# Tile 0 in two transfers with eight gains ahead, four zero writes behind the tables, and the ones-matmuls of the first norm behind the first token tile

## The chip, the cores and the metric

The kernel runs on one core of one Trainium2 chip. The metric is device time in microseconds (us) of one execution; of three runs of the kernel before, the median is 1820.84 us, the lowest 1819.13 and the highest 1823.46.

## What is computed

Two layers of a transformer block over 512 tokens of 1024 channels, in float32. Each layer normalises its input, projects it with one wide matrix into three kinds of attention and gates, merges them, and runs a squared-ReLU MLP; only the first norm and the first projections matter here:

```python
def _rms_norm(x, g):
    x32 = x.astype(jnp.float32)
    y = x32 * lax.rsqrt(jnp.mean(x32 * x32, axis=-1, keepdims=True) + NORM_EPS)
    return (y * g.astype(jnp.float32)).astype(x.dtype)
...
    for l in range(DEPTH):
        h = _rms_norm(x, attn_norm[l])
        proj = h @ w_in[l]
        a_q, a_k, a_v, b_ql, b_kvl, b_kr, c_q, c_k, c_v, gate = jnp.split(proj, IN_SPLITS, axis=-1)

        aq = _partial_rope(_rms_norm(a_q.reshape(grp), a_q_norm[l]), cos_p, sin_p)
        ak = _partial_rope(_rms_norm(a_k.reshape(grp), a_k_norm[l]), cos_p, sin_p)
        o_a = _dilated_mixture(aq, ak, a_v.reshape(grp)).reshape(B, S, DSA_OUT)
...
        x = x + merged @ w_out[l]

        h2 = _rms_norm(x, mlp_norm[l])
        x = x + jnp.square(jax.nn.relu(h2 @ w_ff1[l])) @ w_ff2[l]
    return x
```

## The kernel before

`x` lies transposed: eight tiles of 128 channels by 512 tokens. Every float32 matmul is made of three (`mm3`): both operands are split into a rounded high part and the rest, and high x high (L339), high x low (L340) and low x high (L341) are summed in one accumulator. Weights come in chunks through the SP queue into `raww` (two buffers); ACT casts a chunk to its high part `hl` (three buffers) and DVE subtracts to get the low part, both at a raised priority. The very first chunk is loaded and split in two halves of 128x512.

The norm is not applied ahead of the projection. `norm_tile` multiplies each tile by its gain and splits it (`a`), and sums the squares over the eight tiles in one tile. `norm_steps` splits that sum, multiplies it by a matrix of ones on TensorE (L458, L459, "the ones-matmuls", into `pso`), adds the epsilon on DVE (L461, `tmp`), picks the diagonals out of it (`dg` and `sm`, L468: a custom DVE operation on `tmp` and `ident`) and takes the reciprocal root on ACT and DVE (L358 to L362). The result `rcol` has one factor per token; it scales the projections when ACT empties their accumulators ("evacuations", `raw<-psd,rcol`).

The first projection (`denseB`, queries and keys of the first attention) takes four chunks of weights, each with two channel tiles: 24 matmuls of 512 columns a chunk, over four token tiles with an accumulator each, two of tag d and two of tag s. In its last chunk, the ones-matmuls stand behind token tile `npos`. Each of the four accumulators is emptied twice (two copies of `raw`), so eight evacuations follow. The next projection (288 columns, three channel tiles in its first two chunks) uses tags d, d, d and o; as there are three accumulators of tag d, its second one of tag d needs one that the first projection has given back.

Tile 0 comes with all gains of both layers in one transfer on the ACT queue (128x938 values). Its two operations on DVE are L434 and L435; the other tiles use ACT and DVE (L350, L351). GpSimd (POOL in the profile) writes zeros into the unused halves of the two block diagonal key tiles (`kbd_open`: four casts, L573 and L574, `kT<-zero`), and multiplies the rope tables by gains (L553, `tqb`, `tkb`, `tqn`, `tkn`, `tqr`, `tkr`), which needs the transfer of `ropes`.

Each engine runs its instructions in program order. That order is made when the program is built, by a scheduler that takes what is ready, by priority; `high_priority` raises it, and `issue_after` holds an instruction back in the order until another has been placed.

Of the kernel before, what the change touches and what calls it, by code (L numbers as in the profile page):

```python
# [8 lines left out]
F32 = mybir.dt.float32  # L9
# [3 lines left out]
ALU = mybir.AluOpType  # L13
# [3 lines left out]
P = 128  # L17
L = 2
D = 1024
S = 512  # L20
KT = D // P
NT = S // P
# [141 lines left out]
NG = 21 + 192  # L164
# [91 lines left out]
class Kern:  # L256
# [124 lines left out]
    def setup(self, es):  # L381
        tc, nc = self.tc, self.nc
        self.cp = es.enter_context(tc.tile_pool(name="cp", bufs=1))
        self.kp = es.enter_context(tc.tile_pool(name="kp", bufs=1))
        self.pp = es.enter_context(tc.tile_pool(name="pp", bufs=2, space=PSUM))
        self.wsetup()
        self.x = []
        k = lambda shape, nm, dt=F32: self.kp.tile(shape, dt, name=nm, tag=nm)
        self.bcol = k([96, L, 2], "bcol")
        self.warm(k)  # L390
        x0 = k([P, S + L * NG], "x0")
        nc.scalar.dma_start(x0, self.ins["x0g"])
        nc.scalar.add_instruction(
            mybir.InstLoadActFuncSet(name=nc.get_next_instruction_name(), act_func_set_id=ACT_SET, ins=[], outs=[])
        )
        self.gain = x0[:, S:].rearrange("p (l n) -> p l n", l=L)
        self.x.append(x0[:, :S])
        self.wload(1)
        for j in range(1, KT):
            xt = self.t(self.cp, "x2", [P, S])  # L400
            nc.sync.dma_start(xt, self.ins["xT"][j])
            self.x.append(xt)
            if j == 1:
                self.wload(2)
        self.ident = k([P, P], "ident")
        self.ropes = k([P, NROPE], "ropes")
        self.masks = k([P, NMASK], "masks", BF16)
        self.maskA = self.masks[:, C_MA : C_MA + 256]
        self.maskR = self.masks[:, C_MR : C_MR + 256]
        self.maskB = self.masks[:, C_MB : C_MB + 512]  # L410
        self.resetC = self.masks[:, C_MC : C_MC + 512]
# [16 lines left out]
    def norm_tile(self, j, x):  # L428

        nc = self.nc  # L430
        g = self.gain[:, self.gl, self.goff + j : self.goff + j + 1]
        hl = self.t(self.cp, "a4", [P, 2, S], F32R)
        if j == 0 and self.gl == 0 and self.goff == 0:
            nc.vector.tensor_scalar(hl[:, 0], x, g, None, ALU.mult)  # L434
            nc.vector.scalar_tensor_tensor(hl[:, 1], x, g, hl[:, 0].bitcast(F32), ALU.mult, ALU.subtract)  # L435
        else:
            self.split(hl[:, 0], hl[:, 1], x, g)
        self.xg[j] = hl
        first = self.nacc is None
        if first:  # L440
            self.nacc = self.t(self.cp, "x2", [P, S])
        sq = self.nacc if first else self.t(self.cp, "tmp", [P, S])
        nc.scalar.activation(sq, x, AF.Square)
        if not first:
            nc.vector.tensor_tensor(self.nacc, self.nacc, sq, ALU.add)
# [5 lines left out]
    def norm_steps(self, cols):  # L451

        nc = self.nc
        hl = self.t(self.cp, "a4", [P, 2, S], F32R)
        self.split(hl[:, 0], hl[:, 1], self.nacc)
        yield
        ps = self.ps("o")
        nc.tensor.matmul(ps, self.onesr, hl[:, 0], start=True, stop=False)  # L458
        nc.tensor.matmul(ps, self.onesr, hl[:, 1], start=False, stop=True)  # L459
        a = self.t(self.cp, "tmp", [P, S])  # L460
        nc.vector.tensor_scalar(a, ps, 1.0 / D, EPS, ALU.mult, ALU.add)  # L461
        if cols:
            self.rcol = self.kp.tile([P, 8], F32, tag="rcol", name=self.nm("rcol"))
            c = self.small()
            for i in range(2):
                for t in range(NT):
                    sl = slice(t, None, 4) if i else slice(t * P, t * P + P)
                    nc.vector.tensor_tensor_reduce(  # L468
                        out=self.t(self.kp, "dg", [P, P]), in0=a[:, sl], in1=self.ident, op0=ALU.mult, op1=ALU.add,
                        scale=1.0, scalar=0.0, accum_out=c[:, 4 * i + t : 4 * i + t + 1],  # L470
                    )
                self.rsqrt(self.rcol[:, 4 * i : 4 * i + 4], c[:, 4 * i : 4 * i + 4], self.kp, "sm8", [P, 4])
        self.rrep = self.kp.tile([P, S], F32, tag="rrep", name=self.nm("rrep"))
        self.rsqrt(self.rrep, a, self.cp, "tmp", [P, S])
# [14 lines left out]
    def denseB(self, names, nk, n, evac, res=False, tags="dddo", last=None):  # L489

        pss = [self.ps(tags[t]) for t in range(NT)]
        k0 = 0
        for name, m in zip(names, nk):
            fin = last if name is names[-1] else None
            if fin is not None:
                next(fin)
                if self.gl:
                    for _ in fin:
                        pass
                    fin = None  # L500
            w = self.wget(name)
            for t in range(NT):
                sl = slice(t, None, 4) if res else slice(t * P, t * P + P)
                for kk in range(m):
                    xg = self.xg[k0 + kk]
                    c = kk * n
                    self.mm3(
                        pss[t][:, :n], xg[:, 0, sl], xg[:, 1, sl], w[:, 0, c : c + n], w[:, 1, c : c + n],
                        k0 + kk == 0, k0 + kk == KT - 1,
                    )  # L510
                if fin is not None and t == self.npos:
                    for _ in fin:
                        pass
                if k0 + m == KT and (fin is None or t >= self.npos):
                    for u in range(t + 1) if fin is not None and t == self.npos else (t,):
                        evac(u, pss[u])
            k0 += m


# [25 lines left out]
    def rope_tab(self, base, hf, grow, tag, pool=None):  # L545

        nc = self.nc
        w = 2 * hf  # L550
        src = self.ropes[:, base : base + 8 * w].rearrange("p (t c) -> p t c", t=4)
        t = (pool or self.tp).tile([P, 4, 2 * w], F32, tag=tag, name=self.nm(tag))
        nc.gpsimd.tensor_tensor(t, src, grow.unsqueeze(1).to_broadcast([P, 4, 2 * w]), ALU.mult)  # L553
        return t[:, :, 0:w], t[:, :, w : 2 * w]

    def to_qT(self, y, g, d=P):
# [239 lines left out]
    def layer(self, l):  # L796
        nc, tc = self.nc, self.tc
        st = {}
        g = lambda a, b: self.gain[:, l, a:b]
# [15 lines left out]
        def thread_A():  # L815
            with tc.tile_pool(name=f"ta{l}", bufs=1) as tp:
# [2 lines left out]
                tabs["kn"] = self.rope_tab(R_N, 8, g(53, 85), "tkn")  # L819
                tabs["qr"] = self.rope_tab(R_R, 8, g(21, 53), "tqr")  # L820
                tabs["kr"] = self.rope_tab(R_R, 8, g(53, 85), "tkr")
                self.kbd_open(2)
                yield ("open", "A")
                oA = [self.t(self.cp, "a4", [P, 2, S], F32R) for _ in range(2)]
                st["oA"] = oA
# [438 lines left out]
        for name, cost, fn, need in items:  # L1264
# [10 lines left out]
            while credit > 0:  # L1275
                c = step()
# [18 lines left out]
        for q in range(4):  # L1295
            u = []
# [32 lines left out]
        return self.ins["xT"][j] if l == 0 else self.park[j]  # L1329

    nwarm = 8
    npos = 2
    ratio = 0.8
    w0at = (0, 2, 4)
    srtmp = True
# [50 lines left out]
```

## Time and profile before

| | |
|---|---|
| median of three runs | 1820.84 us |
| profiled execution | 1820.94 us |
| its span, first to last instruction | 1819.1 us |
| granted TensorE clock, mean | 1.000 |
| four zero writes on POOL | 1.94 to 6.25 us |
| first real matmul | 6.68 us |
| first matmul of the next projection | 30.39 us |
| six tables on POOL | 22.68 to 25.47 us |

The profile is of one execution. Its page gives the busy time of each engine and the chain that ended last; the trace also answers with timelines (start and duration of each instruction, in us from the start of the span, and in brackets how long its engine stood idle before it and what ended that), with the waits of an engine, and with busy times in chosen stretches. PE is TensorE, and a matmul's duration overlaps with the next one's, so rates are read from the distance of their starts.

### The profile page before, as it was taken

The page shows a single profiled execution, that of the slowest core. Times are in us where ns is not written, and L with a number is a line of the kernel's source. Part 1 is how long each engine was busy: PE and PEld are TensorE (multiplying, and loading weights), DVE is VectorE, ACT ScalarE, POOL GpSimd, SP SyncE. Part 2 cuts the span into 40 slices and gives each one's busy share as a digit, 9 for nine tenths or more (in the row PEclk, how much of TensorE's full clock was granted, in tenths as well). Part 3 has the DMA queues.
Part 4 walks back from the last instruction along what each step waited for, and adds up shares of the span by engine and source line. Part 5 has one row for each costly group of instructions (what it writes and reads, how often), then busy time and mean ns, then how long its engine had stood idle before and what let it go on. Part 6 is the DMA issues. An engine that isn't in the chain of part 4 may idle for free.

```text
span 1819.1 us, 23060 instructions
## 1 busy us (share of the span) xinstructions
PE 1798.3 (99%) x8592; PEld 1511.8 (83%) x8592; DVE 1158.5 (64%) x2137; ACT 929.8 (51%) x1743; POOL 41.3 (2%) x70
## 2 busy tenths in 40 slices
PE   9999999999999999999999999999999999999999
PEld 8999888777788888888889988887778888888887
DVE  7666799868875443434566558997888654434342
ACT  6646677767744332323446366677767342323241
POOL 1000000000000000000020000000000000000000
PEclk9999999999999999999999999999999999999999
DMA  5222241223353233233432222423234532333332
GB/s 180 83 94 86 65 134 60 97 95 109 116 184 100 93 96 102 93 99 99 133 102 83 91 70 71 133 64 105 93 116 124 171 94 93 101 96 93 104 94 93
DMA packets 64704, 186.78 MB, mean 103 GB/s; under 512 B 11472, under 2 KB 11856, under 8 KB 64592
## 3 DMA queue, kind: packets, MB, share of 16 engines
q1 hardware_dynamic: 57744, 178.35, 30.8%
q0 software_dynamic: 1952, 6.29, 1.0%
q8 instruction: 68, 1.11, 0.2%
q10 hardware_dynamic: 4896, 0.66, 0.2%
q14 instruction: 44, 0.36, 0.1%
HBM read 168.45 MB, written 16.78 MB: 102 GB/s over the span
## 4 chain that ended last, share of the span: by engine, by line
PE 86%; DVE 8%; ACT 4%; issue 1%; DMA 1%; ACTq 0%; SPq 0%; DVEq 0%
PE psd L486 21%; PE psd L485 21%; PE psd L484 21%; PE psd L339 3%; PE psd L341 3%; PE psd L340 3%; PE pst L761 2%; DVE SN L978 1%; PE pss L339 1%; PE pss L340 1%; PE pss L341 1%; DVE hl L251 1%; PE pss L970 1%; PE pst L561 1%; PE pso L742 1%
## 5 line engine op out<-in xcount | busy, mean ns | idle before, releaser
L251 ACT CAST hl<-raww 128x1024 fp32r<-128x1024 f32 (+3 forms) x287 | 298.7, 1041 | 648.4 <-PE psd L486 482.5
L484 PE MATMUL psd<-a,hl 128*128 128x512 f32 x1232 | 484.9, 394 | 0.6 <-DVE VS L251 0.5
L485 PE MATMUL psd<-a,hl 128*128 128x512 f32 x1232 | 484.4, 393 | 0.0
L486 PE MATMUL psd<-a,hl 128*128 128x512 f32 x1232 | 484.4, 393 | 0.0
L251 DVE TENSOR_TENSOR hl<-raww,hl 128x1024 fp32r<-128x1024 f32 (+3 forms) x287 | 347.5, 1211 | 150.8 <-ACT hl L251 150.4
L484 PEld LDWEIGHTS psd<-a,hl 128*128 128x128 f32 x1232 | 231.9, 188 | 45.0 <-DVE VS L251 1.1
L485 PEld LDWEIGHTS psd<-a,hl 128*128 128x128 f32 x1232 | 231.7, 188 | 44.5 <-issue 0.3
L486 PEld LDWEIGHTS psd<-a,hl 128*128 128x128 f32 x1232 | 231.8, 188 | 44.2
L486 PE MATMUL psd<-u,hl 128*128 128x512 f32 (+1 forms) x648 | 250.7, 387 | 0.0
L485 PE MATMUL psd<-u,hl 128*128 128x512 f32 (+1 forms) x648 | 250.7, 387 | 0.0
L484 PE MATMUL psd<-u,hl 128*128 128x512 f32 (+1 forms) x648 | 250.7, 387 | 0.0
L1319 DVE TENSOR_TENSOR x<-x,psd 128x512 f32<-128x512 f32 x63 | 43.3, 688 | 185.0 <-PE psd L486 185.0
L484 PEld LDWEIGHTS psd<-u,hl 128*128 128x128 f32 x648 | 121.8, 188 | 24.7
L485 PEld LDWEIGHTS psd<-u,hl 128*128 128x128 f32 x648 | 121.8, 188 | 24.6
L486 PEld LDWEIGHTS psd<-u,hl 128*128 128x128 f32 x648 | 121.8, 188 | 24.5
L1300 DVE SCALAR_TENSOR_TENSOR tmp<-psd,rrep 128x512 f32<-128x512 f32 x64 | 44.3, 692 | 151.4 <-PE psd L486 151.4
L339 PE MATMUL psd<-hl,a 128*128 128x512 f32 (+3 forms) x328 | 122.6, 375 | 4.5 <-DVE gt L251 2.2
L340 PE MATMUL psd<-hl,a 128*128 128x512 f32 (+3 forms) x328 | 122.0, 372 | 0.0
L341 PE MATMUL psd<-hl,a 128*128 128x512 f32 (+3 forms) x328 | 121.6, 371 | 0.0
L251 ACT ACTIVATE gt<-gt 128x512 f32<-128x512 f32 x144 | 90.0, 628 | 25.5 <-DVE gt L251 20.1
L339 PEld LDWEIGHTS psd<-hl,a 128*128 128x128 f32 x328 | 79.4, 242 | 9.9 <-DVE gt L251 3.0
L340 PEld LDWEIGHTS psd<-hl,a 128*128 128x128 f32 x328 | 79.5, 243 | 3.7
(234 smaller groups left out, 2403.3 us busy)
## 6 DMA issues: line engine op xcount, KB each, us to landing
raww<-w SPq DMA_DIRECT2D x277, 512.0 KB, 3.5
gpark<-gt SPq DMA_DIRECT2D x48, 256.0 KB, 2.3
gt<-gpark SPq DMA_DIRECT2D x48, 256.0 KB, 3.7
x<-xT POOLq DMA_DIRECT2D x8, 256.0 KB, 4.1
park<-x POOLq DMA_DIRECT2D x8, 256.0 KB, 2.3
x<-park POOLq DMA_DIRECT2D x8, 256.0 KB, 3.7
x<-xT SPq DMA_DIRECT2D x7, 256.0 KB, 5.8
outT<-x SPq DMA_DIRECT2D x7, 256.0 KB, 2.0
```

The lines of the kernel that those rows point to most:

```text
L251: return f(*a, **k)
L339: mm(ps, ah, bh, start=start, stop=False)
L340: mm(ps, ah, bl, start=False, stop=False)
L341: mm(ps, al, bh, start=False, stop=stop)
L484: self.nc.tensor.matmul(o, w[:, 0, c : c + P], t[:, 0], start=k == 0, stop=False)
L485: self.nc.tensor.matmul(o, w[:, 0, c : c + P], t[:, 1], start=False, stop=False)
L486: self.nc.tensor.matmul(o, w[:, 1, c : c + P], t[:, 0], start=False, stop=k == last)
L561: nc.tensor.transpose(ps[:d, t * P : t * P + P], y[:, t], self.ident)
L742: mm(po[a, r::4], vr[r // 2][:, r % 2, 2 * hh + g], prs[r // 2][:, c : c + P], start=False, stop=False)
L761: nc.tensor.transpose(ps[:, kt * P : kt * P + P], s[:, kt * P : kt * P + P], self.ident)
L1300: nc.vector.scalar_tensor_tensor(t, ps, 0.0, self.rrep, ALU.max, ALU.mult)
L1319: nc.vector.tensor_tensor(x, x, ps, ALU.add)
```

## The change

The host array `x0g` holds the eight gains of the first norm of layer 0 and then tile 0 (128x520). It is loaded in two transfers, 128x264 and 128x256, both on the ACT queue. All gains come in a transfer of their own (`gain`, 128x426) on the SP queue, behind the last token tile. The two DVE operations on tile 0 are made for each half of its columns. The four zero writes of layer 0 are held back behind the last of the six tables (in layer 1 their order was so already). `npos` is 0, the other token tiles of the last chunk are held back behind the ones-matmuls, and the evacuations are written behind the loop.

```diff
--- before.py
+++ after.py
@@ -388,13 +388,15 @@
         k = lambda shape, nm, dt=F32: self.kp.tile(shape, dt, name=nm, tag=nm)
         self.bcol = k([96, L, 2], "bcol")
         self.warm(k)
-        x0 = k([P, S + L * NG], "x0")
-        nc.scalar.dma_start(x0, self.ins["x0g"])
+        x0 = k([P, KT + S], "x0")
+        self.cut = KT + S // 2
+        for c in (slice(0, self.cut), slice(self.cut, KT + S)):
+            nc.scalar.dma_start(x0[:, c], self.ins["x0g"][:, c])
         nc.scalar.add_instruction(
             mybir.InstLoadActFuncSet(name=nc.get_next_instruction_name(), act_func_set_id=ACT_SET, ins=[], outs=[])
         )
-        self.gain = x0[:, S:].rearrange("p (l n) -> p l n", l=L)
-        self.x.append(x0[:, :S])
+        self.gain0 = x0[:, :KT]
+        self.x.append(x0[:, KT:])
         self.wload(1)
         for j in range(1, KT):
             xt = self.t(self.cp, "x2", [P, S])
@@ -402,6 +404,8 @@
             self.x.append(xt)
             if j == 1:
                 self.wload(2)
+        self.gain = k([P, L, NG], "gain")
+        nc.sync.dma_start(self.gain, self.ins["gain"])
         self.ident = k([P, P], "ident")
         self.ropes = k([P, NROPE], "ropes")
         self.masks = k([P, NMASK], "masks", BF16)
@@ -428,11 +432,13 @@
     def norm_tile(self, j, x):
 
         nc = self.nc
-        g = self.gain[:, self.gl, self.goff + j : self.goff + j + 1]
+        start = self.gl == 0 and self.goff == 0
+        g = self.gain0[:, j : j + 1] if start else self.gain[:, self.gl, self.goff + j : self.goff + j + 1]
         hl = self.t(self.cp, "a4", [P, 2, S], F32R)
-        if j == 0 and self.gl == 0 and self.goff == 0:
-            nc.vector.tensor_scalar(hl[:, 0], x, g, None, ALU.mult)
-            nc.vector.scalar_tensor_tensor(hl[:, 1], x, g, hl[:, 0].bitcast(F32), ALU.mult, ALU.subtract)
+        if start and j == 0:
+            for c in (slice(0, S // 2), slice(S // 2, S)):
+                nc.vector.tensor_scalar(hl[:, 0, c], x[:, c], g, None, ALU.mult)
+                nc.vector.scalar_tensor_tensor(hl[:, 1, c], x[:, c], g, hl[:, 0, c].bitcast(F32), ALU.mult, ALU.subtract)
         else:
             self.split(hl[:, 0], hl[:, 1], x, g)
         self.xg[j] = hl
@@ -456,7 +462,7 @@
         yield
         ps = self.ps("o")
         nc.tensor.matmul(ps, self.onesr, hl[:, 0], start=True, stop=False)
-        nc.tensor.matmul(ps, self.onesr, hl[:, 1], start=False, stop=True)
+        self.sqprod = nc.tensor.matmul(ps, self.onesr, hl[:, 1], start=False, stop=True)
         a = self.t(self.cp, "tmp", [P, S])
         nc.vector.tensor_scalar(a, ps, 1.0 / D, EPS, ALU.mult, ALU.add)
         if cols:
@@ -499,6 +505,7 @@
                         pass
                     fin = None
             w = self.wget(name)
+            pin = ExitStack()
             for t in range(NT):
                 sl = slice(t, None, 4) if res else slice(t * P, t * P + P)
                 for kk in range(m):
@@ -511,9 +518,12 @@
                 if fin is not None and t == self.npos:
                     for _ in fin:
                         pass
-                if k0 + m == KT and (fin is None or t >= self.npos):
-                    for u in range(t + 1) if fin is not None and t == self.npos else (t,):
-                        evac(u, pss[u])
+                    pin.enter_context(self.tc.issue_after(self.sqprod.ins))
+                if k0 + m == KT and fin is None:
+                    evac(t, pss[t])
+            pin.close()
+            for t in range(NT) if fin is not None else ():
+                evac(t, pss[t])
             k0 += m
 
 
@@ -550,7 +560,7 @@
         w = 2 * hf
         src = self.ropes[:, base : base + 8 * w].rearrange("p (t c) -> p t c", t=4)
         t = (pool or self.tp).tile([P, 4, 2 * w], F32, tag=tag, name=self.nm(tag))
-        nc.gpsimd.tensor_tensor(t, src, grow.unsqueeze(1).to_broadcast([P, 4, 2 * w]), ALU.mult)
+        self.lastrope = nc.gpsimd.tensor_tensor(t, src, grow.unsqueeze(1).to_broadcast([P, 4, 2 * w]), ALU.mult)
         return t[:, :, 0:w], t[:, :, w : 2 * w]
 
     def to_qT(self, y, g, d=P):
@@ -819,7 +829,8 @@
                 tabs["kn"] = self.rope_tab(R_N, 8, g(53, 85), "tkn")
                 tabs["qr"] = self.rope_tab(R_R, 8, g(21, 53), "tqr")
                 tabs["kr"] = self.rope_tab(R_R, 8, g(53, 85), "tkr")
-                self.kbd_open(2)
+                with tc.issue_after(self.lastrope.ins):
+                    self.kbd_open(2)
                 yield ("open", "A")
                 oA = [self.t(self.cp, "a4", [P, 2, S], F32R) for _ in range(2)]
                 st["oA"] = oA
@@ -1329,7 +1340,7 @@
         return self.ins["xT"][j] if l == 0 else self.park[j]
 
     nwarm = 8
-    npos = 2
+    npos = 0
     ratio = 0.8
     w0at = (0, 2, 4)
     srtmp = True
@@ -1369,7 +1380,8 @@
     arrays = {
         "xT": xT,
         "w": _pack_weights(a["w_in"], a["w_q_b"], a["w_kv_b"], a["w_branch"], a["w_out"], a["w_ff1"], a["w_ff2"]),
-        "x0g": np.concatenate([xT[0], gain.reshape(P, -1)], axis=1),
+        "x0g": np.concatenate([gain[:, 0, :KT], xT[0]], axis=1),
+        "gain": gain,
         "bcol": _pack_bcols(a["b_q_norm"], a["b_k_norm"]),
         "ident": np.eye(P, dtype=np.float32),
         "ropes": _ropes(),
```

On TensorE, in the last chunk of the first projection; before (`psd` and `pss` are the accumulators of the four token tiles, `hl` the weights, `a4` the channel tiles):

```order
L339 MATMUL pss_45_202<-hl_47_228,a4_27_157 128x512
L340 MATMUL pss_45_202<-hl_47_228,a4_27_157 128x512
L341 MATMUL pss_45_202<-hl_47_228,a4_27_157 128x512
L339 MATMUL pss_45_202<-hl_47_228,a4_29_163 128x512
L340 MATMUL pss_45_202<-hl_47_228,a4_29_163 128x512
L341 MATMUL pss_45_202<-hl_47_228,a4_29_163 128x512
L458 MATMUL pso_53_310<-a4_50_284,onesr_69 128x512
L459 MATMUL pso_53_310<-a4_50_284,onesr_69 128x512
L339 MATMUL pss_46_203<-hl_47_228,a4_27_157 128x512
L340 MATMUL pss_46_203<-hl_47_228,a4_27_157 128x512
L341 MATMUL pss_46_203<-hl_47_228,a4_27_157 128x512
L339 MATMUL pss_46_203<-hl_47_228,a4_29_163 128x512
```

And now, with the first six of the eighteen matmuls that used to stand ahead:

```order
L341 MATMUL psd_43_205<-hl_47_233,a4_27_162 128x512
L339 MATMUL psd_43_205<-hl_47_233,a4_29_168 128x512
L340 MATMUL psd_43_205<-hl_47_233,a4_29_168 128x512
L341 MATMUL psd_43_205<-hl_47_233,a4_29_168 128x512
L464 MATMUL pso_53_303<-a4_50_289,onesr_69 128x512
L465 MATMUL pso_53_303<-a4_50_289,onesr_69 128x512
L339 MATMUL psd_44_206<-hl_47_233,a4_27_162 128x512
L340 MATMUL psd_44_206<-hl_47_233,a4_27_162 128x512
L341 MATMUL psd_44_206<-hl_47_233,a4_27_162 128x512
L339 MATMUL psd_44_206<-hl_47_233,a4_29_168 128x512
L340 MATMUL psd_44_206<-hl_47_233,a4_29_168 128x512
L341 MATMUL psd_44_206<-hl_47_233,a4_29_168 128x512
```

The ones-matmuls (`onesr`) moved 12 matmuls up, behind the first token tile.

On TensorE, where the next projection (`x288`) takes the accumulator of tag d that the first one must give back (`psd_115`), 33 matmuls into it before:

```order
L339 MATMUL pso_117_514<-hl_51_287,a4_19_134 128x288
L340 MATMUL pso_117_514<-hl_51_287,a4_19_134 128x288
L341 MATMUL pso_117_514<-hl_51_287,a4_19_134 128x288
L339 MATMUL pso_117_514<-hl_51_287,a4_21_140 128x288
L340 MATMUL pso_117_514<-hl_51_287,a4_21_140 128x288
L341 MATMUL pso_117_514<-hl_51_287,a4_21_140 128x288
L339 MATMUL psd_115_512<-hl_48_255,a4_11_109 128x288
L340 MATMUL psd_115_512<-hl_48_255,a4_11_109 128x288
L341 MATMUL psd_115_512<-hl_48_255,a4_11_109 128x288
```

and 17 matmuls into it now:

```order
L339 MATMUL pso_117_519<-hl_48_260,a4_14_124 128x288
L340 MATMUL pso_117_519<-hl_48_260,a4_14_124 128x288
L341 MATMUL pso_117_519<-hl_48_260,a4_14_124 128x288
L339 MATMUL pso_117_519<-hl_48_260,a4_16_130 128x288
L340 MATMUL pso_117_519<-hl_48_260,a4_16_130 128x288
L339 MATMUL psd_115_517<-hl_48_260,a4_11_112 128x288
L340 MATMUL psd_115_517<-hl_48_260,a4_11_112 128x288
L341 MATMUL psd_115_517<-hl_48_260,a4_11_112 128x288
L339 MATMUL psd_115_517<-hl_48_260,a4_14_124 128x288
```

The accumulator is taken 16 matmuls sooner; what stood ahead of it, chunk `hl_51` among it, stands behind it.

On GpSimd, from its first cast on, before:

```order
L573 CAST kT_39_192<-zero_65 64x2x512
L574 CAST kT_39_192<-zero_65 64x2x512
L573 CAST kT_40_195<-zero_65 64x2x512
L574 CAST kT_40_195<-zero_65 64x2x512
L553 ISA
L553 TENSOR_TENSOR tqb_33_177<-ropes_103,x0_80 128x256
L553 TENSOR_TENSOR tkb_34_179<-ropes_103,x0_80 128x256
L553 TENSOR_TENSOR tqn_35_184<-ropes_103,x0_80 128x128
L553 TENSOR_TENSOR tkn_36_186<-ropes_103,x0_80 128x128
L553 TENSOR_TENSOR tqr_37_188<-ropes_103,x0_80 128x128
L553 TENSOR_TENSOR tkr_38_190<-ropes_103,x0_80 128x128
```

and now:

```order
L563 TENSOR_TENSOR tqb_33_182<-ropes_106,gain_103 128x256
L563 TENSOR_TENSOR tkb_34_184<-ropes_106,gain_103 128x256
L563 TENSOR_TENSOR tqn_35_189<-ropes_106,gain_103 128x128
L563 TENSOR_TENSOR tkn_36_191<-ropes_106,gain_103 128x128
L563 TENSOR_TENSOR tqr_37_193<-ropes_106,gain_103 128x128
L563 TENSOR_TENSOR tkr_38_195<-ropes_106,gain_103 128x128
L583 CAST kT_39_197<-zero_65 64x2x512
L584 CAST kT_39_197<-zero_65 64x2x512
L583 CAST kT_40_200<-zero_65 64x2x512
L584 CAST kT_40_200<-zero_65 64x2x512
L720 CAST PT_243_1433<-zero_65 128x2x128
```

The four zero writes moved from ahead of the six tables to behind them.

## The prediction

> **What bounds the kernel now.** I read the page first: busy shares, then the chain that ended last.
>
> ```profile
> span 1819.1 us, 23060 instructions
> PE 1798.3 (99%) x8592; PEld 1511.8 (83%) x8592; DVE 1158.5 (64%) x2137; ACT 929.8 (51%) x1743; POOL 41.3 (2%) x70
> PE 86%; DVE 8%; ACT 4%; issue 1%; DMA 1%; ACTq 0%; SPq 0%; DVEq 0%
> ```
>
> TensorE is busy for 99% of the span, so the kernel is bound by its matmuls, and whatever keeps TensorE from its next matmul is paid in full. The profiled execution took 1820.94 us, 1.8 us more than its span; the median of the runs is 1820.84 us, 0.1 less, so I add my sum to 1820.94. The order of the program differs only in its first part (some 300 of 7,890 rows on TensorE), so next I asked for TensorE's waits in the first 100 us.
>
> ```profile
> PE psd L339 <- ACT hl L251: 1.8, 1, 1.8
> PE psd L339 <- ACT raw L251: 0.5, 1, 0.5
> PE psd L484 <- DVE VS L251: 0.5, 1, 0.5
> ```
>
> There are three waits (us in total, times, longest): at the first real matmul, at one that needs an emptied accumulator of the first projection, and at the first matmul of the other form (weights stationary, L484) behind it. Nothing that the change does can take away more than these and what the clock costs at the start. The timeline of TensorE places the first two, and shows the rates I need:
>
> ```profile
> 6.68 1.19 PE L339 MATMUL psd<-hl,a 128*128 128x512 f32 x2 [1.84 <-ACT hl L251]
> 7.67 0.63 PE L339 MATMUL pss<-hl,a 128*128 128x512 f32 x1
> 8.09 1.06 PE L340 MATMUL psd<-hl,a 128*128 128x512 f32 x2
> ...
> 9.71 0.39 PE L340 MATMUL pss<-hl,a 128*128 128x512 f32 x1
> 9.93 0.39 PE L341 MATMUL psd<-hl,a 128*128 128x512 f32 x1
> ...
> 13.58 0.39 PE L339 MATMUL psd<-hl,a 128*128 128x512 f32 x1
> ...
> 28.78 0.39 PE L459 MATMUL pso<-a,onesr 128*128 128x512 f32 x1
> ...
> 30.39 0.29 PE L339 MATMUL psd<-hl,a 128*128 128x288 f32 x1
> ...
> 34.63 0.29 PE L341 MATMUL pso<-hl,a 128*128 128x288 f32 x1
> 35.42 0.40 PE L339 MATMUL psd<-hl,a 128*128 128x288 f32 x1 [0.49 <-ACT raw L251]
> ```
>
> Columns are start, duration, instruction, and in brackets the wait. From 7.67 to 8.09 a 512-column matmul takes 0.42 us, from 9.71 to 9.93 only 0.22 (0.228 on the mean of the 16 steps from 9.93 to 13.58): TensorE ran at half speed until about 9.6. The first 24 end at 13.58. From 30.39 to 34.63 lie 32 steps of 288 columns, 0.1325 each.
>
> **Part 1: an earlier start.** The first matmul waits for its weights (ACT's cast) and for tile 0 times its gains (DVE's L434); the rows are from the timelines of ACT, GpSimd (POOL) and DVE, the last from the DMA issues (KB, us to landing):
>
> ```profile
> 4.98 0.62 ACT L251 CAST hl<-raww 128x512 fp32r<-128x512 f32 x1 [2.50 <-DMA raww<-w]
> ...
> 5.21 1.04 POOL L574 CAST kT<-zero 64x1024 fp32r<-64x1024 f32 x1
> ...
> 5.29 1.24 DVE L434 TENSOR_SCALAR a<-x 128x512 fp32r<-128x512 f32 x1 [4.03 <-DMA x<-x0g]
> ...
> 53.54 0.42 DVE L251 TENSOR_SCALAR gt<-gt 128x512 f32<-128x512 f32 x1
> ...
> x<-x0g ACTq DMA_DIRECT2D x1, 469.0 KB, 4.5
> ```
>
> The cast ends at 5.60. L434 took 1.24 us where a tensor_scalar of the same size takes 0.42: it began under the last of the four zeros on GpSimd (to 6.25) and ended 0.28 after it. The change removes both things: no zero stands there, and half a tile (0.42 / 2) lands sooner, as 132 KB go ahead instead of 469. So the cast is what ends last, and the first matmul starts near 5.6, 1.0 to 1.1 us sooner. If TensorE comes to full speed at the same instant, 9.6, then 1.06 us at half speed are worth 0.5 us. If the shorter idle time ahead of it brings full speed as early as 6.2, two matmuls run at half speed until 6.5 and 22 behind them take 22 x 0.228 = 5.0, so the 24 end near 11.5 instead of 13.58: 2.1 us. I take 1.3, between the two. The additional instructions (two more on DVE, one issue on ACT, one gain transfer on SP behind the last token tile) are under DVE's backlog and the full queues; the bytes ahead of the third weight chunk are the same in sum, 132 + 128 + 213 KB. If that cover is gone they cost the half-tile instructions' fixed time, some 0.2 us.
>
> **Part 2: product of squares 12 matmuls sooner.** The two ones-matmuls move from behind 18 matmuls of the last chunk to behind 6: 12 x 0.228 = 2.7 us. With part 1 the second ends at 29.17 - 2.7 - 1.3 = 25.2. Without anything else in the way the DVE chain behind it would follow as it does now:
>
> ```profile
> 17.16 0.68 DVE L445 TENSOR_TENSOR x<-x,tmp 128x512 f32<-128x512 f32 x1
> ...
> 25.66 1.07 DVE L251 TENSOR_TENSOR hl<-raww,hl 128x864 fp32r<-128x864 f32 x1 [2.76 <-ACT hl L251]
> 29.20 0.69 DVE L461 TENSOR_SCALAR tmp<-pso 128x512 f32<-128x512 f32 x1 [2.48 <-PE pso L459]
> 29.93 0.29 DVE L468 CUSTOM_DVE_ANT_0 dg<-tmp,ident 128x128 f32<-128x128 f32 x1
> ...
> 31.59 0.75 DVE L251 TENSOR_TENSOR hl<-raww,hl 128x576 fp32r<-128x576 f32 x1
> ...
> 33.61 0.16 DVE L362 SCALAR_TENSOR_TENSOR rcol<-sm,sm 128x4 f32<-128x4 f32 x1
> ```
>
> It takes 4.6 us from L461 to rcol at 33.77, with a weight split of 0.75 us inside it. In the new order the split of 1.07 falls there in its place, so I count 4.9: rcol at about 30.1, 3.7 us sooner.
>
> **Part 3: what must wait for it moves up.** With all evacuations behind the loop, TensorE meets the accumulator that the fourth evacuation frees 16 matmuls sooner, 16 x 0.1325 = 2.1 us of work that now stands behind the wait instead of ahead of it.
>
> ```profile
> 33.80 0.47 ACT L251 ACTIVATE raw<-psd,rcol 128x256 f32<-128x256 f32 x1 [1.63 <-DVE rcol L362]
> ```
>
> Before, rcol at 33.77 released TensorE at 35.42: 1.65 later (four evacuations). So the new release, carried to the same matmul, is rcol + 1.65 + 2.1; it is 35.42 when rcol is 31.65. Everything queued behind that matmul on TensorE waits too. The third wait above (0.5, for a DVE result) goes when TensorE arrives later. The whole change is therefore **rcol - 31.65 - 0.5**.
>
> **Part 4: the zeros behind the tables.** They leave the start, but come to lie here:
>
> ```profile
> 22.68 0.71 POOL L553 TENSOR_TENSOR tqb<-ropes,x 128x256 f32<-128x256 f32 x1 [16.43 <-DMA masks<-masks]
> ...
> 25.43 0.39 POOL L710 CAST PT<-zero 128x256 fp32r<-128x256 f32 x1
> ```
>
> The tables still start with the rope transfer, 22.68, and end near 25.45; then come four zeros of 1.04, so GpSimd is busy from 22.7 to 29.7 at least, just when DVE works on the chain of part 2. What that does was seen at L434, and layer 1, whose order is already tables then zeros, shows it again:
>
> ```profile
> 914.75 1.50 POOL L573 CAST kT<-zero 64x1024 fp32r<-64x1024 f32 x1
> ...
> 915.28 1.52 DVE L445 TENSOR_TENSOR x<-x,tmp 128x512 f32<-128x512 f32 x1
> ...
> 918.70 1.69 DVE L251 TENSOR_TENSOR hl<-raww,hl 128x1024 fp32r<-128x1024 f32 x1 [0.29 <-ACT hl L251]
> 919.35 1.94 POOL L574 CAST kT<-zero 64x1024 fp32r<-64x1024 f32 x1
> ```
>
> The L445 of 915.28 (0.68 alone, by the row of 17.16) ends 0.55 after the zero ahead of it, which ends at 916.25; the zero of 919.35 (1.04 alone) ends 0.9 after the DVE operation of 918.70, which ends at 920.39. They take turns, whole instructions at a time. There it costs nothing, since TensorE did not wait. Here each zero can hold the chain once. Nothing shows whether the `dg` operations and the 4-column ones are held. If all are: dg, zero, dg, zero, dg, zero, weight split, zero, dg and so on from 25.45, rcol at 34.2, 4.1 late. If only the long ones are, three zeros meet a waiting DVE operation (the split and two of 0.68) with some 0.6 us of theirs to go: rcol at 32.0, 1.9 late. Less than nothing it cannot be, as no zero does work for this chain; nothing at all is the first rival. I take 33.5, nearer the upper end, as the L434 row and the layer-1 rows held every DVE operation that they met. Sum: 33.5 - 31.65 - 0.5 = **+1.35**, and between the two ends -0.15 and +2.05.
>
> The Trainium skill, "SBUF — State Buffer", section "SBUF: two separate sides", calls the port pair of GpSimd and DVE an exclusive lock held for a whole instruction, also by a DVE operation with two SBUF inputs. The rows above agree with it (1.24 us against 0.42); by it `dg`, which reads two tiles, is held too, and the sum would be +2.05.
>
> **The rivals.** *Little contention (faster).* rcol at 30.1 lets TensorE wait about half a microsecond only, and the start's gain stays: 30.1 - 31.65 - 0.5 = -2.05, between -1.2 and -2.9 with the start's two ends (0.5 and 2.1 in place of 1.3): 1818.9. For it: two-input work is only part of the chain. Against it: the rows of layer 1. The point from which it decides is rcol at 32.15.
>
> *The clock falls in the wait (slower).* In the forecast TensorE, which would be at its waiting matmul at 34.63 + 0.13 - 2.1 - 1.3 = 31.4, stands until 33.5 + 1.65 = 35.15, some 3.8 us, where the longest wait after the start is now 1.26:
>
> ```profile
> 1815.23:1818.64 3.41, 0.41 (x4) 0.20 (x2) 0.42 (x1) 0.00 (x0) 0.00 (x0) 1.00 0.11 38
> 1818.64:1819.10 0.46, 0.00 (x0) 0.00 (x0) 0.00 (x0) 0.00 (x0) 0.00 (x0) 0.50 0.00 0
> ...
> 203.52 0.33 PE L704 MATMUL pst<-ident,SN 128*128 128x128 f32 x1 [1.26 <-DVE SN L605]
> ```
>
> The first two rows are windows at the program's end (busy time of PE, PEld, DVE, ACT, POOL, then the granted clock): after 3.41 us with only 0.41 of TensorE's work the clock fell to 0.50. The wait of 1.26 in the last row did not lower it. 3.8 us lie nearer the first. At half speed for half to one and a half such stretches behind the wait, 1.7 to 5.2 us, TensorE loses 0.9 to 2.6, mean 1.7: 1.35 + 1.7 = +3.1, 1824.0, and up to +4.7. It decides from a wait of about 3.4 us. The Trainium skill, "TensorE: Matmul & The Clock Gate", Part 1, gives one idle window of about 3.4 us, on a grid that runs freely, as what halves the clock; the first two rows agree with that length, 3.41. By it a wait of 3.8 us seldom holds a whole idle window, and the sum would stay at +1.35.
>
> *The start does not come sooner,* because the cast or its transfer is later than I think. With the chain held by GpSimd the sum has no term of the start left, so the time is the forecast's, 1822.3.
>
> **How the numbers follow.** Forecast, chain held and clock kept: 0.52 (with the start that stays put in it), 1820.94 + 1.35 = 1822.3, own range 1820.4 to 1823.2. Little contention: 0.25, 1818.9. Clock falls: 0.23, 1824.0. The runs of before lie 4.3 us apart, so a median may be off by 1. Eight in ten then reach from 1818.5 to 1825.2. About 0.2%, 3.6 us, is what a measurement of this kernel can tell from no change: faster by more needs every gain at its bound, 0.04; slower by more needs the fallen clock with its upper half, 0.13; within, 0.83.
>
> **What would show it.** First matmul at 5.6 instead of 6.68, the tensor_scalar of tile 0 as two of 0.2 to 0.3 us: part 1. The second ones-matmul ending near 25.2: part 2. Zeros between 25.4 and 32 with durations over 1.04, DVE's `dg` over 0.29 and rcol at 33.5: part 4. A TensorE wait of 3 to 4.5 us on ACT's evacuations at the third accumulator of 288 columns: part 3. Matmuls of 288 columns 0.26 apart behind it: the clock. rcol before 31 would make the forecast wrong, and so would an evacuation whose release TensorE does not wait for.

## The result and the profile after

The changed kernel took 1837.25 us (median of five runs, 1836.69 to 1837.93) against 1820.8 us (1819.13 to 1823.46): 0.9% slower, ratio 1.0091 with a 95% interval of 1.0078 to 1.0103. That is some 15 us more than was forecast and outside the range. The page after, its span and its first line of busy times:

```profile
span 1835.5 us, 23060 instructions
PE 1813.6 (99%) x8592; PEld 1512.4 (82%) x8592; DVE 1162.2 (63%) x2139; ACT 928.9 (51%) x1743; POOL 42.6 (2%) x70
```

The span grew by 16.4 us, and TensorE's *busy* time by 15.3, with the same 8592 matmuls. Waits account for little: this is TensorE doing the same work more slowly. First the part of which the prediction spoke. Two of TensorE's waits in the first 60 us after (total, times, longest), and its timeline:

```profile
PE psd L339 <- ACT raw L251: 3.7, 1, 3.7
PE psd L340 <- DVE hl L251: 0.4, 1, 0.4
```

```profile
4.66 1.19 PE L339 MATMUL psd<-hl,a 128*128 128x512 f32 x2
...
34.53 0.61 PE L339 MATMUL psd<-hl,a 128*128 128x288 f32 x1 [3.68 <-ACT raw L251]
34.94 0.44 PE L340 MATMUL psd<-hl,a 128*128 128x288 f32 x1
35.18 0.44 PE L341 MATMUL psd<-hl,a 128*128 128x288 f32 x1
...
48.86 0.50 PE L490 MATMUL psd<-a,hl 128*128 128x512 f32 x1 [0.42 <-DVE VS L251]
```

The wait at the first matmul is gone, the wait for the evacuations is 3.68 us (3.8 was forecast), and behind it matmuls of 288 columns stand 0.24 apart instead of 0.1325. The last row is the first matmul with stationary weights; the kernel before has it earlier:

```profile
44.51 0.50 PE L484 MATMUL psd<-a,hl 128*128 128x512 f32 x1 [0.47 <-DVE VS L251]
```

So the changed kernel is 4.35 us late there; further on, from some 200 us to the MLP, 3.4 us of it are left (the first matmul on the MLP's `u` tiles starts at 522.8 instead of 519.4). DVE and GpSimd after, from their timelines:

```profile
25.92 1.10 POOL L583 CAST kT<-zero 64x1024 fp32r<-64x1024 f32 x1
27.08 1.04 POOL L584 CAST kT<-zero 64x1024 fp32r<-64x1024 f32 x1
28.18 1.75 POOL L583 CAST kT<-zero 64x1024 fp32r<-64x1024 f32 x1
29.97 1.04 POOL L584 CAST kT<-zero 64x1024 fp32r<-64x1024 f32 x1
...
26.17 1.00 DVE L474 CUSTOM_DVE_ANT_0 dg<-tmp,ident 128x128 f32<-128x128 f32 x1
...
27.10 1.93 DVE L251 TENSOR_TENSOR hl<-raww,hl 128x864 fp32r<-128x864 f32 x1
28.95 1.12 DVE L474 CUSTOM_DVE_ANT_0 dg<-tmp,ident 128x128 f32<-128x128 f32 x1
...
30.00 1.55 DVE L360 SCALAR_TENSOR_TENSOR tmp<-tmp 128x512 f32<-128x512 f32 x1
...
32.72 0.15 DVE L362 SCALAR_TENSOR_TENSOR rcol<-sm,sm 128x4 f32<-128x4 f32 x1
```

`dg` takes 1.00 and 1.12 instead of 0.29, the split 1.93 instead of 1.07, L360 1.55 instead of 0.68: four DVE operations each wait out a zero, and the third zero (1.75) waits out the split. rcol is ready at 32.87. The granted clock (1.00 is full speed), in windows of TensorE's work (length, busy with count, clock, DMA share, GB/s):

```profile
30.25:33.66 3.41, 0.60 (x5) 1.00 0.41 142
33.67:37.08 3.41, 2.55 (x10) 0.50 0.32 90
37.08:40.50 3.42, 3.42 (x16) 0.50 0.16 63
```

It fell to 0.50 after a stretch with 0.60 us of work, for two stretches of 3.41; the 5.97 us that TensorE worked in them are worth some 3.0 at full speed, so about 3.0 of the early loss is the clock. The rest of the loss lies where nothing was edited. Two stretches of 40 us of layer 1's MLP, the first multiplying the channel tiles `a`, the second the `u` tiles (the squared-ReLU results). In both, that tile is the moving one, streamed past the weights `hl`; in a row, the moving tile is the first name behind the arrow. Before, then after:

```profile
1555.00:1595.00 40.00, 40.00 (x178) 1.00 0.30 92
1599.00:1639.00 40.00, 40.00 (x178) 1.00 0.31 93
```

```profile
1568.00:1608.00 40.00, 40.00 (x178) 1.00 0.30 92
1612.00:1652.00 40.00, 40.00 (x173) 1.00 0.31 93
```

TensorE is never idle in any of them, the clock is 1.00 and the transfers move as much, but on `u` it gets through 173 matmuls instead of 178. Of the 648 x 3 = 1944 matmuls on `u`, 1,896 have 512 columns. From start to start their mean is 233.3 ns instead of 226.7; on `a` it stays near 228. 1896 x 6.7 ns = 12.7 us, and with some 3.5 us from the start that is nearly all of the 16.4.

What differs for `u`? Its place in SBUF, the on-chip memory from which the engines read their tiles. Tile `x0` with all gains had 3752 bytes per partition; now `x0` has 2080 and `gain` 1704, together 3784. Everything allocated behind them lies 32 bytes further: `u` begins at byte 152480 instead of 152448. The weights `hl` (from 84096) and the channel tiles (from 30848), allocated ahead, did not move.

### The profile page after: what moved, and what is told of

Same layout as the page of the kernel before. It is cut to its first block, busy times and chain, and to the rows that moved or that the text cites. A ratio compares the mean times of both kernels' runs of the same rounds, so it can differ in the third digit from the quotient of the medians.

```text
span 1835.5 us, 23060 instructions
## 1 busy us (share of the span) xinstructions
PE 1813.6 (99%) x8592; PEld 1512.4 (82%) x8592; DVE 1162.2 (63%) x2139; ACT 928.9 (51%) x1743; POOL 42.6 (2%) x70
## 3 DMA queue, kind: packets, MB, share of 16 engines
q1 hardware_dynamic: 57888, 178.57, 30.4%
## 4 chain that ended last, share of the span: by engine, by line
PE 86%; DVE 8%; ACT 4%; issue 1%; DMA 1%; ACTq 0%; DVEq 0%
PE psd L492 21%; PE psd L490 21%; PE psd L491 21%; PE psd L339 3%; PE psd L340 3%; PE psd L341 3%; PE pst L771 2%; DVE SN L989 1%; PE pss L339 1%; PE pss L341 1%; PE pss L340 1%; DVE hl L251 1%; PE pss L981 1%; PE pst L571 1%; PE pso L752 1%
## 5 line engine op out<-in xcount | busy, mean ns | idle before, releaser
L490 PE MATMUL psd<-u,hl 128*128 128x512 f32 (+1 forms) x648 | 254.2, 392 | 0.0
L492 PE MATMUL psd<-u,hl 128*128 128x512 f32 (+1 forms) x648 | 254.2, 392 | 0.0
L491 PE MATMUL psd<-u,hl 128*128 128x512 f32 (+1 forms) x648 | 254.1, 392 | 0.0
```

The costliest lines, as they stand in the source:

```text
L490: self.nc.tensor.matmul(o, w[:, 0, c : c + P], t[:, 0], start=k == 0, stop=False)
L491: self.nc.tensor.matmul(o, w[:, 0, c : c + P], t[:, 1], start=False, stop=False)
L492: self.nc.tensor.matmul(o, w[:, 1, c : c + P], t[:, 0], start=False, stop=k == last)
```

## The experiments

Two questions: what slows the matmuls on `u`, and what makes the early loss. Each time is compared with runs of the kernel before on the same chip (medians 1820.0 to 1820.5 us).

**Padding, first round.** Thirty-two bytes more behind `gain` in the changed kernel, and 32 or 64 behind `x0` in the kernel before:

```diff
-        self.gain = k([P, L, NG], "gain")
+        gt = k([P, L * NG + 8], "gain")
+        self.gain = gt[:, : L * NG].rearrange("p (l n) -> p l n", l=L)
```

```diff
-        x0 = k([P, S + L * NG], "x0")
-        nc.scalar.dma_start(x0, self.ins["x0g"])
+        x0 = k([P, S + L * NG + 8], "x0")
+        nc.scalar.dma_start(x0[:, : S + L * NG], self.ins["x0g"])
...
-        self.gain = x0[:, S:].rearrange("p (l n) -> p l n", l=L)
+        self.gain = x0[:, S : S + L * NG].rearrange("p (l n) -> p l n", l=L)
```

The other paddings differ in the number of columns alone: 16 for 64 bytes, 24 for 96, 56 for 224.

> The changed kernel with 32 more bytes per partition behind the gain tile and nothing else, so that every tile allocated behind it begins again at a multiple of 64 bytes. Theory A (a matmul whose moving operand begins 32 bytes off a multiple of 64 is slower: 1944 matmuls on the u tiles at 233.3 instead of 226.7 ns, 12.8 us): the matmuls on u come back to 0.227 us and the time is 1837.25 - 12.8 = 1824.4. Rival B (the later part is slower for something else in the change, as the new gain transfer or its tile): stays near 1837. What is left over 1820.8 in A, about 3.5, is the wait for the evacuations and the clock behind it.

Measured: 1827.09 us, ratio 1.0039 (1.0027 to 1.0052). Its early part, in the profiled execution, differs from that of the changed kernel, though the order is the same. TensorE starts at 4.86, but at half speed until about 10.6, and begins its 25th matmul at 13.52, no sooner than before the change (13.58; 11.43 in the changed kernel). The wait for the evacuations is shorter:

```profile
PE psd L339 <- ACT raw L251: 2.1, 1, 2.1
```

The clock stays at 1.00 behind it, and the first matmul on `u` starts at 520.8, only 1.4 us later than before.

> The kernel before, with 32 unused bytes per partition behind tile x0 and nothing else. A: 1820.8 + 12.8 = 1833.6, matmuls on u at 0.233. B: 1820.8, no change.

Measured: 1833.02 us, ratio 1.0071 (1.0057 to 1.0085).

> The kernel before, with 64 unused bytes there. A: no change, 1820.8, since all tiles keep their place modulo 64. A rival to A in which any shift of the tiles is what costs (a boundary that a tile crosses): slower by several us.

Measured: 1824.57 us, ratio 1.0025 (1.0015 to 1.0035).

Thirty-two unused bytes alone make the kernel before 12.8 us slower, as theory A says, so the term is one of place and not of the new transfer. But 64 bytes, which should be free by A, cost 4.3 us, and the matmuls on `u` take 229.0 ns in both kernels with that offset. A falls in its form: it is not a multiple of 64 that matters.

> The kernel before, with the eight u tiles of a quarter of the MLP begun at byte 0, 32, 64, 16, 48, 8, 4 and 0 of a larger buffer, all else unchanged. A: within one quarter the matmuls on the tiles at 0 and 64 keep 226.7 ns and those on 32 take 233; if it is the multiple of 64 that counts, those at 16, 48, 8 and 4 take as long as 32, and the time is about 1820.8 + 1536 x 5/8 x 0.0066 = 1827.1. If only 32-byte places matter (0 and 64 against 32 and 48, say), less. B: all alike, 226.7.

```diff
-                ut = self.t(self.fp, "u4", [P, 2, S], F32R)
+                ut = self.t(self.fp, "u4", [P, 2 * S + 16], F32R)
+                o = (0, 8, 16, 4, 12, 2, 1, 0)[j]
+                ut = ut[:, o : o + 2 * S].rearrange("p (i n) -> p i n", i=2)
```

Measured: 1833.22 us in one run, and all matmuls on `u` slow. It does not do what it was meant to: each buffer is 64 bytes longer, so the tiles moved by other amounts than the list. Sorted by the distance that each tile really had from the weights (modulo 256), the mean steps go from 230.0 ns (at 128) to 236.7 (at 72), and are 232.2 at a multiple of 256. It fits neither A nor B, and the theory that comes out below does not explain it.

**Padding to 128 bytes, and the parts of the early loss.** The next four have 96 bytes behind `gain`, so `u` lies 128 bytes further than before; three of them undo or replace a part. "The tie" stands for the ones-matmuls behind the first token tile with all evacuations behind the loop.

> The changed kernel with 96 more bytes per partition behind the gain tile and nothing else: all tiles behind it lie where the kernel before has them plus 128 bytes. Theory A2 (what counts is the start of the moving tile modulo 128: 0 gave 226.7 ns, 64 gave 229.0, 32 gave 233.3): matmuls on u at 226.7 ns, time 1837.25 - 1944 x 0.0066 = 1824.4, or by the run with 32 bytes 1827.09 - 1944 x 0.0023 = 1822.6. Rival (any shift costs, or 64 was as good as it gets): u stays at 229 and the time at 1827. What is left over 1820.3 is the wait for the evacuations, +1 to +4 with the fallen clock.

Measured: 1836.42 us, ratio 1.0083 (1.0069 to 1.0097): a plain miss. The matmuls on `u` are back at 233.3 ns. So 128 is as bad as 32, and modulo 128 falls too. What these four say of the early part is read from their traces ahead of the MLP, and from their times less the 12.8 us; for this run that is 1823.6, 3.2 above the kernel before (1820.46).

> As the run with 96 bytes, and the four zero writes back in their old place ahead of the tables (the rest of the change kept). Theory H (the zeros hold the chain to rcol): rcol at about 30.5, no long wait at the third 288-column accumulator, but tile 0 is again held for up to 1 us by the zeros; by the forecast's sum 30.5 - 32.15 = -1.7, 1818.6. Rival T (the earlier ones-matmuls with all evacuations behind the loop make the wait): the wait of 3.7 us stays and the time is that of the run with 96 bytes, about 1822.6.

```diff
-                with tc.issue_after(self.lastrope.ins):
-                    self.kbd_open(2)
+                self.kbd_open(2)
```

Measured: 1833.39 us, with the 12.8 us of the place in it. DVE and TensorE:

```profile
4.15 1.18 DVE L441 TENSOR_SCALAR a<-x 128x256 fp32r<-128x256 f32 x1 [2.89 <-DMA x<-x0g]
...
7.46 0.50 PE L340 MATMUL psd<-hl,a 128*128 128x512 f32 x1 [1.28 <-DVE hl L251]
...
30.22 0.16 DVE L362 SCALAR_TENSOR_TENSOR rcol<-sm,sm 128x4 f32<-128x4 f32 x1
...
43.96 0.50 PE L491 MATMUL psd<-a,hl 128*128 128x512 f32 x1 [0.26 <-DVE VS L251]
```

With the zeros ahead of the tables rcol comes at 30.4, 2.5 us sooner than in the changed kernel, the evacuations are waited for no more than 0.2 us, and the checkpoint of 44.51 is reached at 43.96. The zeros cost again at the start (1.18 for half a tile instead of 0.35). The tie is kept here, so rival T falls. H's time does not come out: less the 12.8 the run takes 1820.6, not 1818.6. The profiled execution is the fastest of the five, 1830.96; in it the first matmul on `u` is 1.7 us ahead of the kernel before, as H said.

> As the run with 96 bytes, and the four zero writes put where all three engines still wait for the first transfers: two on POOL, one on ACT, one on DVE, all done by about 4.1 us (one to two of the first transfers are issued at the same place as in the changed kernel). H: first matmul near 4.7, rcol near 29.7, wait at the third accumulator under 1 us, -2.5: 1817.8. T: as above, about 1822.

Measured: 1831.98 us, with the same 12.8 us in it: less these 1819.2, better than T's 1822 but 1.4 over H's 1817.8. It is run again below at a better place.

> As the run with 96 bytes, but npos 2 and the evacuations as before (the tie undone), the zeros still behind the tables. H: the chain begins at about 27.1 and the zeros still hold it, rcol at 33.5 to 34.5, the release for an accumulator that is 16 matmuls later again: +0.2 to -0.8, about 1820. T: the start's gain and nothing lost, -2: 1818.3.

```diff
-    npos = 0
+    npos = 2
...
-                    pin.enter_context(self.tc.issue_after(self.sqprod.ins))
-                if k0 + m == KT and fin is None:
-                    evac(t, pss[t])
-            pin.close()
-            for t in range(NT) if fin is not None else ():
-                evac(t, pss[t])
+                if k0 + m == KT and (fin is None or t >= self.npos):
+                    for u in range(t + 1) if fin is not None and t == self.npos else (t,):
+                        evac(u, pss[u])
```

Measured: 1833.83 us, likewise. Its trace:

```profile
33.67 0.15 DVE L362 SCALAR_TENSOR_TENSOR rcol<-sm,sm 128x4 f32<-128x4 f32 x1
...
35.48 0.40 PE L339 MATMUL psd<-hl,a 128*128 128x288 f32 x1 [2.42 <-ACT raw L251]
```

Undone is the tie: the ones-matmuls are again behind the third token tile and the evacuations within the loop. With the zeros behind the tables rcol is at 33.8 even so, where T expected a clean gain; TensorE, 2 us ahead by then, waits 2.42 and is released at 35.48, as before at 35.42. So the zeros alone eat the start's gain. Less the 12.8 the run takes 1821.0, 0.6 above the kernel before, where the tie made it 3.2: the larger part of the loss needs both. With the tie the wait begins 16 matmuls sooner, and the clock falls in it; here it stayed at 1.00.

**Which place.** Offsets 0, 32, 64 and 128 of `u` gave 226.7, 233.3, 229.0 and 233.3 ns; the channel tiles, whose distance to the weights is a multiple of 256, were always fast, and before the change `u` has such a distance too (152448 - 84096 = 267 x 256). Two theories fit, R and P below.

> The kernel before, with the one-column zero tile allocated ahead of all others: the weights hl, the channel tiles a4 and raww lie 32 bytes further, the u tiles where they were. Theory R (what counts is where the moving tile starts relative to the weights hl, modulo 256: in the kernel before 0 for u and for a4, both fast; 32, 64 and 128 for u are slow): matmuls on a4 stay at 227.7 ns, those on u get slower, by about 2 to 7 ns each, 1824 to 1834. Theory P (the place of the moving tile itself, modulo 256: 128 is fast, 160, 192 and 0 are slow): u stays at 226.7, the some 3700 matmuls on a4 take 6.6 ns more, 1845. Theory W (the place of the weights): both slower.

```diff
-        self.zero = k([P, 1], "zero")
...
+        self.zp = es.enter_context(tc.tile_pool(name="zp", bufs=1))
+        self.zero = self.zp.tile([P, 1], F32, name="zero", tag="zero")
         self.cp = es.enter_context(tc.tile_pool(name="cp", bufs=1))
```

Measured: 1833.83 us, ratio 1.0075 (1.0059 to 1.0090). The same two stretches, on `a` and on `u`:

```profile
1567.00:1607.00 40.00, 40.00 (x178) 1.00 0.34 104
1611.00:1651.00 40.00, 40.00 (x173) 1.00 0.33 98
```

The `u` tiles did not move, and are slow; the channel tiles moved together with the weights, and are fast. P and W fall.

> The kernel before with every tile, weights, channel tiles and u, 32 bytes further. R: no change, 1820.5. P: all matmuls of 512 columns on a4 and u 6.6 ns slower, some 5600 of them, 1857. W: slower as well.

In addition to the edit above, `bcol` takes 32 bytes more, so that `x0` and all behind it move as well. Measured: 1819.89 us, ratio 0.9999 (0.9990 to 1.0008): no change with every tile 32 bytes off, 226.7 ns on `u`. R stands. R still left open which tile of that group it is:

> The kernel before, with the one-column zero tile put between the channel tiles a4 and the weights hl: hl and the small work tiles behind it lie 32 bytes further, while raww, the channel tiles and the u tiles keep their places. Theory R (the place of the moving tile relative to the weight tile that the same matmul reads, modulo 256): matmuls on a4 and on u are both slower, 227 to about 233 ns, 5600 x 0.0066 = 37 us, 1857. Rival (the place relative to other tiles of that pool, raww, x2 or a4, which DVE, ACT and the transfers use meanwhile): no change, 1820.4.

```diff
-        self.zero = k([P, 1], "zero")
-        nc.gpsimd.memset(self.zero, 0.0)
...
             self.norm_tile(j, self.x[j])
+            if j == 0:
+                self.zero = self.cp.tile([P, 1], F32, name="zero", tag="zero", bufs=1)
+                nc.gpsimd.memset(self.zero, 0.0)
```

Measured: 1850.85 us, ratio 1.0167 (1.0150 to 1.0184), with both stretches slow:

```profile
1580.00:1620.00 40.00, 40.00 (x173) 1.00 0.29 92
1624.00:1664.00 40.00, 40.00 (x173) 1.00 0.30 93
```

Both are at 233.3 ns now. It is the weights. The small work tiles behind them moved too, but no such matmul reads these, and what other engines do with them has no part: around 797 of the steps on `u` and 590 on `a`, VectorE, ScalarE and GpSimd all stand idle, and their means are 233.3 as well. The 37 us expected were too many, as `a` began at 228.1: 3,541 steps without a longer gap (under 300 ns) x 5.2 + 1,896 x 6.7 ns = 31 us, against 30.8 measured. That this fits so closely is partly luck, since 408 matmuls the other way round (weights moving, channel tiles loaded) also went from 227.3 to 233.2, another 2.4 us.

**The change at the right distance.** With 224 bytes behind `gain` all lies 256 bytes further:

> The changed kernel with 224 more bytes behind the gain tile: everything behind it 256 bytes further than in the kernel before. R and P alike: period 256, u back to 226.7 ns. The time is then what the rest of the change costs: in the run with 96 bytes the matmuls ahead of the MLP were 2.7 us late with the clock fallen, so 1820.5 + 1 to 3.5 = 1821.5 to 1824. If the period is longer (512 or more), u stays over 229 and the time over 1826.

Measured: 1823.88 us over 11 runs (1821.79 to 1824.55), ratio 1.0017 (1.0008 to 1.0026). `u` is fast again, and the wait with the halved clock behind it remains:

```profile
1559.00:1599.00 40.00, 40.00 (x178) 1.00 0.29 93
1603.00:1643.00 40.00, 40.00 (x178) 1.00 0.31 96
...
29.46:32.87 3.41, 1.50 (x12) 1.26 (x10) 3.41 (x13) 1.18 (x4) 2.04 (x2) 1.00 0.48 154
32.87:36.28 3.41, 1.99 (x8) 1.99 (x9) 1.94 (x8) 3.41 (x12) 0.00 (x0) 0.50 0.17 35
...
34.29 0.61 PE L339 MATMUL psd<-hl,a 128*128 128x288 f32 x1 [3.33 <-ACT raw L251]
```

(The two rows in the middle give the busy time of PE, PEld, DVE, ACT and POOL and then the clock.) So of the 16.4 us the rest of the change makes 3.5, and the 32 bytes the other 12.9. Not every execution pays the 3.5: of the eleven, the only one with a mean clock of 1.000 took 1821.79, and the ten with 0.998 or 0.999 took 1823.10 to 1824.55.

> The run with the zeros spread over POOL, ACT and DVE at the start, with 224 bytes in place of 96. If the period is 256: 1831.98 - 12.8 = 1819.2, and below the kernel before (1820.5) by the 1.3 us that its first matmuls were ahead. If not: over 1825.

```diff
-            nc.gpsimd.tensor_copy(k[0:64, :, 1, :], z[0:64].to_broadcast([64, 2, S]))
-            nc.gpsimd.tensor_copy(k[64:128, :, 0, :], z[64:128].to_broadcast([64, 2, S]))
+            if self.gl == 0 and self.kbds:
+                with self.tc.high_priority(5000):
+                    nc.scalar.copy(k[0:64, :, 1, :], z[0:64].to_broadcast([64, 2, S]))
+                    nc.vector.tensor_copy(k[64:128, :, 0, :], z[64:128].to_broadcast([64, 2, S]))
+            else:
+                nc.gpsimd.tensor_copy(k[0:64, :, 1, :], z[0:64].to_broadcast([64, 2, S]))
+                nc.gpsimd.tensor_copy(k[64:128, :, 0, :], z[64:128].to_broadcast([64, 2, S]))
```

(The first transfers and ACT's table load are given a still higher priority, so that they stay ahead, and the hold behind the tables is taken out.) Measured: 1819.10 us over 11 runs, ratio 0.9992 (0.9983 to 1.0001): 18 us better than the changed kernel, and 1.3 us ahead of the kernel before by the medians, which the interval does not quite part from no change. From its timelines:

```profile
2.96 1.04 ACT L588 CAST kT<-zero 64x1024 fp32r<-64x1024 f32 x1
...
1.29 0.69 DVE L589 CAST kT<-zero 64x1024 fp32r<-64x1024 f32 x1
...
29.77 0.15 DVE L362 SCALAR_TENSOR_TENSOR rcol<-sm,sm 128x4 f32<-128x4 f32 x1
...
31.58 0.40 PE L339 MATMUL psd<-hl,a 128*128 128x288 f32 x1 [0.51 <-ACT raw L251]
...
43.60 0.47 PE L493 MATMUL psd<-a,hl 128*128 128x512 f32 x1 [0.62 <-DVE VS L251]
```

rcol is at 29.92, close to where the prediction put it for a chain that nothing holds (30.1), and the wait is 0.51.

## Why the prediction was wrong

- **The step that failed** is the frame of the sum: "The order of the program differs only in its first part", so the sum has terms for that part alone ("The whole change is therefore **rcol - 31.65 - 0.5**"). An equal order does not make an equal duration. The new `gain` tile was counted as one more transfer, hidden by the full queues; its 32 more bytes per partition were put at nothing, and they cost 12.9 us, nearly all of it in 1,896 matmuls that no line of the diff touches. No rival had it either.
- **Part 1** was right in kind: first matmul at 4.66 instead of the 5.6 forecast. The weights landed sooner too (ACT's cast starts at 3.93 instead of 4.98); that the smaller transfer beside them did it is likely, but was not tried alone. Full speed came before 6.7, and the first 24 ended at 11.43 instead of 13.58: 2.15 us, the upper of the two cases. That it came so soon was luck of this execution: with the same order, the run with 32 bytes came to full speed near 10.6 and gained 0.06.
- **Part 2** and **part 3** held: the ones-matmuls ended near 24.5 (25.2 forecast), and TensorE met its accumulator 16 matmuls sooner and waited there, 3.68 us against 3.8.
- **Part 4** held in mechanism and nearly in size: rcol at 32.87 (33.5), in a chain that began 0.7 sooner than forecast. By the prediction's own sum, 32.87 - 31.65 - 0.5, that is +0.7. The 0.5 was wrong: the third wait did not go, it was 0.42. Without that term the sum is +1.2, and with the 3.0 of the clock 4.2, against the 4.35 measured at that matmul. `dg` is held, which was open; the Trainium skill's "SBUF — State Buffer", "SBUF: two separate sides", had said so for two SBUF inputs against a GpSimd operation that reads SBUF, as these casts read `zero`. Yet the sum did not come to the +2.05 that the prediction tied to this: only two of the `dg` that rcol needs waited out a zero (1.00 and 1.12), and the first two took 0.45 and 0.38.
- **Which case.** Without the 32 bytes the change costs 3.5 us, so not the forecast (+1.35) but the rival with the falling clock (+3.1) describes most of its executions. It was given 0.23. Where the clock held, the forecast fits: +1.4 in the profiled execution of the run with 32 bytes, up to the first matmul on `u`, and +1.4 in the one run with 224 bytes whose mean clock was 1.000. What spoke against the rival was the page "TensorE: Matmul & The Clock Gate" of the Trainium skill, Part 1, with one idle window; here the clock fell after a stretch with 0.60 us of work in 3.41, and in the run with 224 bytes after one with 1.5, so no wholly idle stretch is needed. The prediction's own row had shown that already, with 0.41 us of work in the stretch.

## What to carry to other kernels

A tile that grows moves all tiles behind it. Where a kernel is bound by TensorE, compare the tiles' places before and after a change as carefully as the order, and keep moving tiles and weights at a distance that ran fast (here a multiple of 256 bytes). And a write taken off one engine's critical start is not free elsewhere: ask what DVE does at its new place, and put it where the engines still wait for the first transfer.

## What the runs showed of the hardware

The float32 matmuls of 512 columns on `u` take 226.7 ns from start to start when the moving tile begins a multiple of 256 bytes from the weight tile, and 233.3 when it lies 32 bytes to either side or 128 away, 229.0 at 64. Moving both together changes nothing. On `a`, moving the weights by 32 bytes took the mean from 228.1 to 233.3. Narrower matmuls hardly slowed: in that run the mean step of 384 columns went from 174.5 to 174.2 ns, that of 256 columns on `u` from 119.9 to 118.2, and that of 288 from 132.1 to 133.9. Other types were not tried, and why the distance matters is not shown. The rule does not explain the run with mixed offsets, where tiles at a good distance were slow too (232.2); whether a neighbour's place carries over was not tried.

The clock's changes in each of these traces lie a multiple of 3.41 us apart. Counted in stretches on that grid, a clock at full speed fell after 0.60 (the changed kernel), 1.50 (224 bytes) and 1.51 us of TensorE's work (96 bytes), and held after 1.61 (32 bytes), 1.67 (tie undone) and 1.74 (96 bytes). No other stretch in the fifteen traces speaks against a bound between 1.51 and 1.61. So the same wait can cost the halved clock in one execution and not in the next, by where the grid lies.
